# Latent attention with the keys on the partitions: scores made twice, sums taken by ones beside the values

## The chip, the cores and the metric

The kernel runs on one core of a Trainium2 chip. The metric is the device time of one execution in microseconds (us); the time of a kernel is the median of its runs. Engines are called PE (TensorE), PEld (its weight loads), DVE (VectorE), ACT (ScalarE), POOL (GpSimd) and SP (SyncE, which issues DMAs).

## The reference, cut to what matters

Two layers of a hybrid block run over 512 latent tokens and 256 context tokens of width 1024. In each layer an input projection is split into four head groups, each mixed in its own way; the four results are concatenated, projected out, normed and added, and a gated MLP follows. The change is in the fourth group, multi-head latent attention with 4 heads, 64 + 32 score features and 64 value features a head:

```python
def attend(q, k, v):
    ...
    def block(qblk):
        s = jnp.einsum('bqhd,bkhd->bhqk', qblk, k).astype(F32) * scale
        p = jax.nn.softmax(s, axis=-1).astype(v.dtype)
        return jnp.einsum('bhqk,bkhd->bqhd', p, v)
...
ox = attend(queries(cq_x, True), jnp.concatenate([kc, kx], axis=1), jnp.concatenate([vc, vx], axis=1))
if ctx_out:
    oc = attend(queries(cq_c, False), kc, vc).reshape(...)
```

The latent queries see all 768 keys, the context queries only the 256 context keys. Context outputs are made in the first layer (layer 0) and not in the second (layer 1).

## The kernel before, in words

Activations lie with features on the partitions and tokens in the free dimension. Tokens 0 to 511 are the latent stream (groups 0 and 1 of 256), tokens 512 to 767 the context (group 2). Large products are made of three float32r matmuls (`mm3`, L199 to L201): each operand is split into a high part and the rest, and high x high, low x high and high x low are summed in PSUM. Plain float32 matmuls are used elsewhere; the trace records each of them as two instructions with a weight load each, and a transpose through PE as one.

`mixer_d` is a generator called by `mixers`. Its first part makes the rotated shared keys, the values `V` (tile `dv`, tokens on the partitions, 256 columns for 4 heads) and, with `project(h)`, the split queries (`qh2`, `ql2`: slots of tile `hhx` for heads 0 and 1, tiles `pq` and `pl` for heads 2 and 3) and keys (`kh2`, `kl2` in tiles `hh` and `hl`, two slots, used again by heads 2 and 3). After the `yield` follow the four heads, with `project(2)` after head 0 and `project(3)` after head 1.

`attend(h, qt)` does one block of 128 queries: scores with the queries on the partitions (nine matmuls of 256 columns for a latent block, three for a context block), the maximum along the free dimension on DVE (L1136), the exponential on ACT with the maximum as bias and the sum accumulated (L1138), a reciprocal of 128x1 (L1140), transposes of the probabilities by PE (L1144), their copies out of PSUM by ACT (L1148) and DVE (L1146), the product with the values (L1151, 64 columns) and the scaling by the reciprocal (L1153). `finish(hp)` transposes the outputs of two heads back (L1163), splits them into `hhx` and `hlx` for the output projection (`parts`, L1192 and L1193) and stores the context part. `turn(w)` hands out PSUM tiles by turns: two of two banks (`pe2`, `pd2`) and four of one bank (`pe1` and `pd1`, two buffers each), the whole PSUM.

After the generator, `mixers` loads the results of the other three groups back from DRAM in three pieces through one buffer (`mix`, L1643) and splits them by the same `parts`. They may be split as soon as the last read of the queries of heads 0 and 1 has released `hhx` (`new_hx`, called after head 1). The output projection, with `pf` in PSUM, follows.

The order of instructions on each engine is set by the framework's scheduler: instructions whose inputs are ready in its own timeline are issued by priority, which follows program order, so that work of the next block fills gaps of the one before. Each engine then runs its list in that order and waits at the head of it.

## Time and profile before

| | us |
|---|---|
| median of 3 runs | 1920.27 |
| lowest, highest | 1911.92, 1923.88 |
| the profiled execution, device time | 1919.09 |
| its span in the profile | 1917.0 |
| PE busy (share) | 1777.0 (93%) |
| DVE busy (share) | 1197.3 (62%) |
| ACT busy (share) | 777.2 (41%) |
| mean granted clock of PE | 0.942 |

The profile is of one execution. A busy PE is not a PE at its peak: a row's duration holds the passage through the array, so the pace of a run of matmuls is read from the distance between their starts. The granted clock is a share of 2.4 GHz; 0.50 is the lower level, 1.2 GHz.

### The profile page before, as it was taken

The page shows a single profiled execution, that of the slowest core. Times are in us where ns is not written, and L with a number is a line of the kernel's source. Part 1 is how long each engine was busy: PE and PEld are TensorE (multiplying, and loading weights), DVE is VectorE, ACT ScalarE, POOL GpSimd, SP SyncE. Part 2 cuts the span into 40 slices and gives each one's busy share as a digit, 9 for nine tenths or more (in the row PEclk, how much of TensorE's full clock was granted, in tenths as well). Part 3 has the DMA queues.
Part 4 walks back from the last instruction along what each step waited for, and adds up shares of the span by engine and source line. Part 5 has one row for each costly group of instructions (what it writes and reads, how often), then busy time and mean ns, then how long its engine had stood idle before and what let it go on. Part 6 is the DMA issues. An engine that isn't in the chain of part 4 may idle for free.

```text
span 1917.0 us, 28265 instructions
## 1 busy us (share of the span) xinstructions
PE 1777.0 (93%) x11256; PEld 1523.2 (79%) x11256; DVE 1197.3 (62%) x2200; ACT 777.2 (41%) x1241; POOL 123.5 (6%) x142
## 2 busy tenths in 40 slices
PE   5899999889988999999999988988879999999996
PEld 2785777689977788888888887877669988888886
DVE  8866734655899744774683674792554665454545
ACT  3433454445653332322232354364434653333332
POOL 0000000001420000000000042000000320000002
PEclk9999998889999999999999978998788899999998
DMA  9457630006624332453442323322002622323241
GB/s 351 148 171 248 192 95 23 28 26 214 185 74 131 114 117 95 124 162 94 130 145 89 138 78 114 111 78 88 23 24 81 195 87 81 110 84 110 82 150 44
DMA packets 94387, 222.16 MB, mean 116 GB/s; under 512 B 10928, under 2 KB 41008, under 8 KB 93232
## 3 DMA queue, kind: packets, MB, share of 16 engines
q1 hardware_dynamic: 94256, 220.36, 36.7%
q8 instruction: 89, 1.46, 0.3%
q14 instruction: 42, 0.34, 0.1%
HBM read 193.35 MB, written 24.08 MB: 113 GB/s over the span
## 4 chain that ended last, share of the span: by engine, by line
PE 71%; DVE 12%; issue 10%; ACT 4%; DMA 2%; POOL 1%; SPq 0%; POOLq 0%; DVEq 0%; ACTq 0%
PE pf L199 16%; PE pf L200 16%; PE pf L201 16%; PE pg L199 3%; PE pg L201 3%; PE pg L200 3%; PE pb L243 1%; DVE wlo L192 1%; DVE z L1205 1%; PE pd L1151 1%; PE pn L322 1%; PE pc L704 1%; DVE nu L389 1%; DVE junk L236 1%; DMA bk<-bk 1%
## 5 line engine op out<-in xcount | busy, mean ns | idle before, releaser
L192 DVE TENSOR_TENSOR wlo<-raw,whi 128x1024 fp32r<-128x1024 f32 (+1 forms) x215 | 252.2, 1174 | 299.5 <-ACT whi L191 294.4
L191 ACT ACTIVATE whi<-raw 128x1024 fp32r<-128x1024 f32 (+1 forms) x215 | 217.2, 1011 | 399.4 <-PE pf L200 340.6
L199 PE MATMUL pf<-hhx,whi 128*128 128x512 f32 (+1 forms) x1032 | 363.5, 359 | 11.3 <-DVE z L1205 5.1
L200 PE MATMUL pf<-hlx,whi 128*128 128x512 f32 (+1 forms) x1032 | 368.1, 358 | 5.3 <-DVE hlx L391 5.0
L201 PE MATMUL pf<-hhx,wlo 128*128 128x512 f32 (+1 forms) x1032 | 365.3, 355 | 0.3 <-DVE wlo L192 0.3
L199 PEld LDWEIGHTS pf<-hhx,whi 128*128 128x128 f32 x1032 | 198.2, 195 | 39.3 <-ACT hhx L390 5.7
L200 PEld LDWEIGHTS pf<-hlx,whi 128*128 128x128 f32 x1032 | 200.6, 194 | 33.0 <-DVE hlx L391 8.4
L201 PEld LDWEIGHTS pf<-hhx,wlo 128*128 128x128 f32 x1032 | 200.6, 194 | 26.5 <-DVE wlo L192 0.5
L199 PE MATMUL pf<-g,whi 128*128 128x512 f32 (+1 forms) x552 | 185.4, 342 | 6.0 <-DVE z L1205 3.4
L201 PE MATMUL pf<-g,wlo 128*128 128x512 f32 (+1 forms) x552 | 187.3, 341 | 0.8 <-DVE wlo L192 0.8
L200 PE MATMUL pf<-g,whi 128*128 128x512 f32 (+1 forms) x552 | 187.6, 341 | 0.0
L1205 DVE SCALAR_TENSOR_TENSOR z<-pf,cols,z 128x511 f32<-128x511 f32 (+1 forms) x264 | 167.9, 656 | 24.3 <-ACT z L1203 21.7
L200 PE MATMUL pf<-hl,whi 128*128 128x256 f32 x432 | 123.5, 287 | 1.5 <-DVE hl L391 1.4
L199 PE MATMUL pf<-hh,whi 128*128 128x256 f32 x432 | 121.6, 286 | 1.7 <-ACT hh L390 1.7
L201 PE MATMUL pf<-hh,wlo 128*128 128x256 f32 x432 | 122.6, 285 | 0.0
L199 PEld LDWEIGHTS pf<-g,whi 128*128 128x128 f32 x552 | 104.7, 192 | 19.6 <-issue 4.3
L201 PEld LDWEIGHTS pf<-g,wlo 128*128 128x128 f32 x552 | 105.8, 192 | 12.2 <-DVE wlo L192 1.0
L200 PEld LDWEIGHTS pf<-g,whi 128*128 128x128 f32 x552 | 105.9, 192 | 11.3
L1203 ACT ACTIVATE z<-pf,cols 128x512 f32<-128x512 f32 (+1 forms) x132 | 89.8, 694 | 34.3 <-PE pf L201 29.3
L1284 DVE TENSOR_TENSOR y<-y,pf 128x512 f32<-128x512 f32 (+1 forms) x88 | 44.6, 515 | 73.8 <-PE pf L201 73.6
L125 POOL TENSOR_TENSOR nroy<-nroy,mhalf 128x2 f32<-128x2 f32 x10 | 9.9, 994 | 1211.4 <-DVE nroy L124 896.3
L200 PEld LDWEIGHTS pf<-hl,whi 128*128 128x128 f32 x432 | 83.4, 193 | 3.8 <-DVE hl L391 2.3
(457 smaller groups left out, 3434.1 us busy)
## 6 DMA issues: line engine op xcount, KB each, us to landing
raw<-in_w SPq DMA_DIRECT2D x170, 512.0 KB, 3.6
rawm<-in_wmod SPq DMA_DIRECT2D x64, 512.0 KB, 4.2
raw<-in_w SPq DMA_DIRECT2D x48, 384.0 KB, 3.1
wm<-in_wmod SPq DMA_DIRECT2D x8, 1024.0 KB, 10.1
silu<-in_wmod SPq DMA_DIRECT2D x16, 512.0 KB, 5.8
dx<-g SPq DMA_DIRECT2D x32, 256.0 KB, 2.2
dG<-gt SPq DMA_DIRECT2D x16, 256.0 KB, 2.3
dE<-es SPq DMA_DIRECT2D x16, 256.0 KB, 2.7
```

The source lines that it names most:

```text
L191: nc.scalar.activation(hv, src, AF.Copy)
L192: nc.vector.tensor_tensor(lv, src, hv.bitcast(F32), op=ALU.subtract)
L199: self.nc.tensor.matmul(out, lh, rh, start=i == 0, stop=False)
L200: self.nc.tensor.matmul(out, lh, rl, start=False, stop=False)
L201: self.nc.tensor.matmul(out, ll, rh, start=False, stop=i == n - 1)
L236: self.nc.vector.scalar_tensor_tensor(junk[:], wt, 1.0, self.silu[w][:], op0=ALU.mult, op1=ALU.mult, accum_out=self.modacc[l][:, w, m:m + 1])
L243: self.nc.tensor.matmul(acc[32 * q:32 * q + 2, :], self.ct[:, k, :], halves[q // 2][:, q % 2 * 512:q % 2 * 512 + 512], start=k == 0, stop= ...
L322: self.nc.tensor.matmul(ps[:, j:j + 1], acc[:, k, j * 128:(j + 1) * 128], self.ones[:, 0:1], start=k == 0, stop=k == 1)
L389: nc.vector.scalar_tensor_tensor(u[:], xk, sc, pb, op0=ALU.mult, op1=ALU.mult)
L1203: nc.scalar.activation(z[:, o:o + m], p[:, :m], AF.Identity, bias=b, scale=w1)
L1205: self.last = nc.vector.scalar_tensor_tensor(z[:, o + d:o + d + m - 1], p[:, s:s + m - 1], w, z[:, o + d:o + d + m - 1], op0=ALU.mult, op1 ...
L1284: nc.vector.tensor_tensor(y[:, m, t0:t0 + tw], y[:, m, t0:t0 + tw], ps[:, :tw], op=ALU.add)
```

## The change: what it does

- `attend` is replaced by `maxima(h)` and `values(h)`. `maxima` makes the scores as before, in pieces of 512 and 256 columns, and keeps only the negated maxima (DVE). It turns the six (or four) columns of maxima into one row by PE transposes of a column read 128 times, and writes that row, split into a high and a low part, into partition 96 of the queries. Partition 96 of the keys holds ones in the high part and zeros in the low.
- `values` makes the scores again with the keys on the partitions, 97 rows instead of 96, so that the maximum is subtracted by the matmul itself: per 128 keys three float32r matmuls of 512 queries (256 for context queries), one exponential on ACT, and one float32 matmul with `V` as weights. `V` has 192 columns for a pair of heads, 64 of one head, 64 ones, 64 of the other, so that 128 columns of it give the values in one half of the partitions and the sums of the probabilities in the other.
- After the last keys, DVE takes the reciprocal of the sums (64 partitions x 512) and multiplies. The result has features on the partitions, so the transposes of `finish` go away.
- The sums live in one PSUM bank `po` with one buffer; the one-bank tiles that are handed out by turns are three now instead of four (`pe1` has one buffer).
- New in the first part: a POOL memset for the ones in `V`, two copies instead of one for each piece of `V`, and two DVE copies that write ones and zeros into partition 96 of the keys.
- Order: `maxima` of heads 0 and 1, `values(0)`, `project(2)`, `maxima(2)`, `values(1)`, `project(3)`, `maxima(3)`, `finish(0)`, `values(2)`, `values(3)`, `finish(1)`.

```diff
--- before.py
+++ after.py
@@ -28,7 +28,7 @@
 CHUNKS = [6, 6, 6, 4]
 NCH = T // 8
 KDVE = 5
-PB = 3
+PB = 4
 XK, RK, KS = 4, 7, KT
 AHD = 0
 AHO = 0
@@ -85,7 +85,7 @@
 
 
 WU, NW = w_units()
-TAG_BUFS = {"pg": 2, "pb2": 1, "pb1": 2, "px2": 1, "pc1": 2, "pd2": 1, "pe2": 1, "pe1": 2, "pd1": 2, "pf": 6, "pn": 2, "pn4": 1, "pm": 3}
+TAG_BUFS = {"pg": 2, "pb2": 1, "pb1": 2, "px2": 1, "pc1": 2, "pd2": 1, "pe2": 1, "pe1": 1, "po": 1, "pd1": 2, "pf": 6, "pn": 2, "pn4": 1, "pm": 3}
 
 
 class Net:
@@ -1079,17 +1079,25 @@
         rotate(kr, ps)
         nc.scalar.copy(kr[r0, NX:], ps[r0, NX:T])
 
-        V = self.t(p, [128, 6, 256], "dv")
+
+        V = self.t(p, [128, 6, 2, 192], "dv")
+        nc.gpsimd.memset(V[:, :, :, 64:128], 1.0)
         for i in range(0, 6, 4):
             n = min(4, 6 - i)
             ps = self.turn(2)
             for j in range(n):
                 nc.tensor.matmul(ps[:, j * 256:(j + 1) * 256], ck[:96, (i + j) * 128:(i + j + 1) * 128],
                                  wk[:96, 256:512], start=True, stop=True)
-            nc.scalar.copy(V[:, i:i + n].rearrange("p i c -> p (i c)"), ps[:, :n * 256])
+            pv = ps[:, :n * 256].rearrange("p (i a r c) -> p i a r c", i=n, a=2, r=2)
+            for r in range(2):
+                nc.scalar.copy(V[:, i:i + n, :, r * 128:r * 128 + 64], pv[:, :, :, r, :])
         scale = float(96 ** -0.5)
         qs2 = [self.h_slots("hhx", F32R)[0]] * 2
         kh2, kl2 = (self.h2_slot(x) for x in ("hh2", "hl2"))
+
+        mrow = slice(96, 97)
+        for v, x in ((kh2, self.ones), (kl2, self.zeros)):
+            nc.vector.tensor_copy(v[mrow], x[mrow, 0:1].unsqueeze(2).to_broadcast([1, 2, T]))
 
         def project(h):
             hr = h % 2
@@ -1119,72 +1127,75 @@
 
         ot = {}
 
-        def attend(h, qt):
+        def maxima(h):
 
             hp, hr = h // 2, h % 2
-            qs = slice(qt * 128, (qt + 1) * 128)
-            kg = (0, 1, 2) if qt < 4 else (2,)
-            k0 = kg[0] * 256
-            nk = len(kg) * 256
-            ps = self.turn(2)
             qh2, ql2 = qs2[hp]
-            for g in kg:
-                gs = slice(g * 256, (g + 1) * 256)
-                self.mm3(ps[:, g * 256 - k0:g * 256 - k0 + 256],
-                         [((qh2[:96, hr, qs], ql2[:96, hr, qs]), (kh2[:96, hr, gs], kl2[:96, hr, gs]))])
-            mx = self.t(p, [128, 3], "dmx", bufs=4)
-            nc.vector.tensor_reduce(mx[:, 0:1], ps[:, :nk], axis=AX.X, op=ALU.max, negate=True)
-            pr, pp = (self.t(self.pe, [128, T], x, bufs=PB)[:] for x in ("pr", "pt"))
-            nc.scalar.activation(pr[:, :nk], ps[:, :nk], AF.Exp, bias=mx[:, 0:1],
-                                 accum_out=mx[:, 1:2])
-            nc.vector.reciprocal(mx[:, 2:3], mx[:, 1:2])
-            for a, b in ((0, 384), (384, 768)) if nk == 768 else ((0, 256),):
-                pt = self.turn(1)
-                for j in range(a, b, 128):
-                    nc.tensor.transpose(pt[:, j - a:j - a + 128], pr[:, j:j + 128], self.ident)
-                if a:
-                    nc.vector.tensor_copy(pp[:, a:b], pt[:, :b - a])
-                else:
-                    nc.scalar.copy(pp[:, a:b], pt[:, :b - a])
-            po = pt[:, 384:448]
-            for j in range(nk // 128):
-                nc.tensor.matmul(po, pp[:, j * 128:(j + 1) * 128], V[:, k0 // 128 + j, h * 64:h * 64 + 64],
-                                 start=j == 0, stop=j == nk // 128 - 1)
-            return ts(ot[hp][:, qt, hr * 64:hr * 64 + 64], po, mx[:, 2:3], None, op0=ALU.mult)
-
-        def heads(h):
+            mx = self.t(p, [128, 6], "dmx", bufs=2)
             for qt in range(nq):
-                attend(h, qt)
-
-        def finish(hp):
-
+                qs = slice(qt * 128, (qt + 1) * 128)
+                k0 = 0 if qt < 4 else 512
+                nk = T - k0
+                ps = self.turn(2)
+                for k1, w in ((0, 512), (512, 256))[qt // 4:]:
+                    gs = slice(k1, k1 + w)
+                    self.mm3(ps[:, k1 - k0:k1 - k0 + w],
+                             [((qh2[:96, hr, qs], ql2[:96, hr, qs]), (kh2[:96, hr, gs], kl2[:96, hr, gs]))])
+                nc.vector.tensor_reduce(mx[:, qt:qt + 1], ps[:, :nk], axis=AX.X, op=ALU.max, negate=True)
             ps = self.turn(2)
             for qt in range(nq):
-                nc.tensor.transpose(ps[:, qt * 128:(qt + 1) * 128], ot[hp][:, qt], self.ident)
+                nc.tensor.transpose(ps[:, qt * 128:(qt + 1) * 128], mx[:, qt:qt + 1].to_broadcast([128, 128]), self.ident)
+            nc.scalar.activation(qh2[mrow, hr, :tn], ps[mrow, :tn], AF.Copy)
+            tt(ql2[mrow, hr, :tn], ps[mrow, :tn], qh2[mrow, hr, :tn].bitcast(F32), op=ALU.subtract)
+
+        def values(h):
+
+            hp, hr = h // 2, h % 2
+            qh2, ql2 = qs2[hp]
+            rows, other = slice(hr * 64, hr * 64 + 64), slice(64 - hr * 64, 128 - hr * 64)
+            for q0, nqs, kts in ((0, 512, range(6)), (512, 256, (4, 5)))[:2 if ctx_out else 1]:
+                qs = slice(q0, q0 + nqs)
+                po = self.t(self.pso, [128, 512], "po")
+                for j in kts:
+                    ks = slice(j * 128, (j + 1) * 128)
+                    ps = self.turn(1)
+                    self.mm3(ps[:, :nqs], [((kh2[:97, hr, ks], kl2[:97, hr, ks]), (qh2[:97, hr, qs], ql2[:97, hr, qs]))])
+                    pt = self.t(self.pe, [128, 512], "pt", bufs=PB)
+                    nc.scalar.activation(pt[:, :nqs], ps[:, :nqs], AF.Exp)
+                    nc.tensor.matmul(po[:, :nqs], V[:, j, hp, hr * 64:hr * 64 + 128], pt[:, :nqs],
+                                     start=j == kts[0], stop=j == 5)
+                rec = self.t(self.pe, [128, 512], "rec", bufs=2)
+                nc.vector.reciprocal(rec[rows, :nqs], po[other, :nqs])
+                tt(ot[hp][rows, qs], po[rows, :nqs], rec[rows, :nqs], op=ALU.mult)
+
+        def finish(hp):
+
             for g in range(2):
                 gs = slice(g * 256, g * 256 + 256)
-                self.parts(g, slice(6 + hp, 7 + hp), ps[:, gs].unsqueeze(1))
+                self.parts(g, slice(6 + hp, 7 + hp), ot[hp][:, gs].unsqueeze(1))
             if ctx_out:
-                mix = self.t(p, [128, T], "df")
-                nc.scalar.copy(mix[:, NX:], ps[:, NX:T])
-                store(hp, mix, NX)
+                store(hp, ot[hp], NX)
 
         for h in range(2):
             project(h)
         yield
-        ot[0] = self.t(p, [128, 6, 128], "dot")
-        heads(0)
+        ot[0] = self.t(self.pe, [128, T], "dot", bufs=2)
+        for h in range(2):
+            maxima(h)
+        values(0)
         qs2[1] = [self.t(self.pe, [128, 2, T], x, F32R) for x in ("pq", "pl")]
         project(2)
-        heads(1)
+        maxima(2)
+        values(1)
         self.new_hx()
         for g in range(2):
             self.new_h(g)
         project(3)
+        maxima(3)
         finish(0)
-        ot[1] = self.t(self.pe, [128, 6, 128], "dot")
+        ot[1] = self.t(self.pe, [128, T], "dot", bufs=2)
         for h in (2, 3):
-            heads(h)
+            values(h)
         finish(1)
 
     def parts(self, g, ks, src):
@@ -1635,7 +1646,8 @@
         mxs.__exit__(None, None, None)
         psls.__exit__(None, None, None)
         with self.pool("pse", space=PSUM) as pse, self.pool("me") as self.pe:
-            self.psd = {2: [(pse, "pe2"), (psd, "pd2")], 1: [(pse, "pe1"), (psd, "pd1")]}
+            self.psd = {2: [(pse, "pe2"), (psd, "pd2")], 1: [(pse, "pe1"), (psd, "pd1"), (psd, "pd1")]}
+            self.pso = pse
             next(d, None)
             self.pre = [self.load_w(l, ("out", j), i) for j in range(2) for i in range(2)]
             for k in range(0, 6, 2):
```

## Rows read from the trace of the kernel before

**Rows 1.** The page: busy time of an engine, and the chain by engine.
```profile
PE 1777.0 (93%) x11256; PEld 1523.2 (79%) x11256; DVE 1197.3 (62%) x2200; ACT 777.2 (41%) x1241; POOL 123.5 (6%) x142
...
PE 71%; DVE 12%; issue 10%; ACT 4%; DMA 2%; POOL 1%; SPq 0%; POOLq 0%; DVEq 0%; ACTq 0%
```

**Rows 2.** Stretches: length; PE, PEld, DVE, ACT, POOL busy (instructions); clock; DMA share, GB/s.
```profile
308.00:354.90 46.90, 40.05 (x378) 27.62 (x377) 28.54 (x51) 19.15 (x36) 0.00 (x0) 0.67 0.09 30
...
354.90:440.10 85.20, 76.40 (x543) 70.26 (x541) 50.03 (x110) 41.50 (x92) 0.00 (x0) 0.90 0.07 21
1345.00:1396.50 51.50, 41.77 (x437) 29.46 (x435) 31.52 (x60) 18.72 (x35) 0.61 (x2) 0.73 0.05 17
...
1396.50:1471.40 74.90, 65.08 (x447) 59.34 (x448) 41.24 (x82) 30.48 (x62) 0.00 (x0) 0.85 0.08 25
...
415.00:420.00 5.00, 5.00 (x25) 5.00 (x25) 0.64 (x3) 0.43 (x3) 0.00 (x0) 0.50 0.00 0
```

**Rows 3.** Waits, 355 to 440 then 1395 to 1475: total, times, longest.
```profile
PE pe L1144 <- ACT pr L1138: 6.3, 4, 2.8
...
ACT hhx L1192 <- DMA mix<-dmixr: 2.4, 2, 1.6
...
PE pe L1144 <- ACT pr L1138: 8.9, 4, 2.8
...
ACT hhx L1192 <- DMA mix<-dmixr: 5.3, 2, 4.3
```

**Rows 4.** Timeline of PE in the MLP, first and last of two runs of 18.
```profile
701.84 0.40 PE L199 MATMUL pf<-g,whi 128*128 128x512 f32 x1
...
705.72 0.39 PE L201 MATMUL pf<-g,wlo 128*128 128x512 f32 x1
705.94 0.28 PE L199 MATMUL pf<-g,whi 128*128 128x256 f32 x1
...
707.98 0.28 PE L201 MATMUL pf<-g,wlo 128*128 128x256 f32 x1
```

**Rows 5.** Chain of waits in order of time, layer 0's attention: start, us, what.
```profile
383.52 0.33 PE pe L1144 x3
...
386.27 2.63 PE pd L1151 x24
...
389.81 1.43 PE pe L1099 x4
...
392.34 2.60 PE pd L1111 x8
```

**Rows 6.** DVE by line and shape: busy us, mean ns, idle before.
```profile
L1146 DVE COPY pt<-pd 128x384 f32<-128x384 f32 x32 | 17.7, 552 | 13.4 <-PE pd L1144 13.3
L1136 DVE TENSOR_REDUCE dmx<-pe 128x1 f32<-128x768 f32 x16 | 15.3, 954 | 8.7 <-PE pe L201 8.6
...
L1072 DVE TENSOR_TENSOR hlx<-pd,dcst 32x512 f32<-32x512 f32 x10 | 7.0, 696 | 0.1
L1140 DVE RECIPROCAL dmx<-dmx 128x1 f32<-128x1 f32 x40 | 6.4, 159 | 6.8 <-ACT pr L1138 6.7
L764 DVE COPY s5a<-s5v 64x512 f32<-64x512 f32 x8 | 4.7, 593 | 0.0
...
L947 DVE TENSOR_TENSOR bon<-bon,bry 128x1536 f32<-128x1536 f32 x1 | 1.8, 1757 | 0.0
...
L528 DVE RECIPROCAL eq<-eq 128x32 f32<-128x32 f32 x2 | 0.7, 344 | 0.0
...
L527 DVE TENSOR_TENSOR eq<-eq,ks 128x32 f32<-128x32 f32 x2 | 0.4, 192 | 0.0
```

**Rows 7.** ACT by line and shape, the same columns.
```profile
L1148 ACT COPY pt<-pe 128x384 f32<-128x384 f32 x32 | 15.2, 476 | 27.2 <-PE pe L1144 26.8
L1138 ACT ACTIVATE pr<-pe,dmx 128x768 f32<-128x768 f32 x16 | 14.4, 900 | 18.4 <-DVE dmx L1136 18.1
...
L806 ACT ACTIVATE s5a<-pc,s5hb 128x512 f32<-128x512 f32 x4 | 2.7, 687 | 7.7 <-PE pc L804 7.7
```

## The prediction

> **What bounds the kernel now.** I read the page first: PE is busy 93% of the span and holds 71% of the chain that ended last, DVE 12% [rows 1]. So a change counts by what it does to PE's time, as work or as waiting. Next come the stretches that attention covers [rows 2]: 85.2 us in layer 0 (354.9 to 440.1, first scores to the first output projection) and 74.9 us in layer 1 (1396.5 to 1471.4). The two are 160 us, 8.3% of the time. PE is idle in them for 85.20 - 76.40 = 8.8 and 74.90 - 65.08 = 9.8 us. The mean granted clock is 0.90 and 0.85, that is 17 and 22 us at the lower level (1.2 GHz), and half of that is lost: 8.5 and 11.2 us. Losses in all: 17.3 + 21.0 us. The waits say where the idle time arises [rows 3]: PE waits at the transposes for exponentials, four times a layer, up to 2.8 us. ACT in turn stands at the head of its list waiting for the DMA of `mix`, 2.4 us in layer 0 and 5.3 us in layer 1. After such gaps PE stays at 0.50 for long: from 415 to 420 it was busy all the time and was still granted the lower level [rows 2].
>
> **PE's work, warm.** The paces: a float32r matmul of 512 columns takes (705.72 - 701.84)/17 = 0.228 us, one of 256 (707.98 - 705.94)/17 = 0.120 us [rows 4]. Transposes go at 0.33/3 = 0.11 us, the product with the values at 2.63/24 = 0.110 us an instruction (its 64 columns take as long as a transpose's 128, so the weight load sets that pace). `project`'s eight query instructions, four of 512 and four of 256, take 2.60 us: 0.433 and 0.217 us each [rows 5]. These last are the price of the new float32 product, which streams 512 columns in two instructions.
>
> Per head in layer 0, before: 42 score matmuls 5.04, 28 transposes 3.08, 56 product instructions 6.14, 3 transposes of `finish` 0.33; sum 14.6 us. After: `maxima` 4 x 3 x (0.228 + 0.120) + 2 x 3 x 0.120 = 4.90, six transposes 0.66, second scores 18 x 0.228 + 6 x 0.120 = 4.82, product 12 x 0.433 + 4 x 0.217 = 6.06; sum 16.4. That is +1.8 a head, +7.3 for the layer. In layer 1, without context queries: 12.4 before (4.32 + 2.64 + 5.26 + 0.22), 13.9 after (4.18 + 0.44 + 4.10 + 5.20), +5.9 for the layer. **PE gains 13.2 us of work.** As a check on the paces: layer 0's four heads and the two projections inside (each 1.3 for keys, from the 1.43 of the row, and 2.6) come to 66.2 us warm; 85.2 less this is 19.0 us lost, near the 17.3 above.
>
> **The other engines.** Removed on DVE: 40 small reciprocals, 32 copies of 0.55, 40 scalings. On ACT, 40 sums and 40 copies of up to 0.48 go away, and the exponential of 0.90 per 128 latent queries [rows 6, 7]. Added on ACT: 48 exponentials of 128x512 at 0.69, 8 of half that width, and a row copy a head; ACT gets lighter. Its 0.69 per 128 keys lies beside 3 x 0.228 + 2 x 0.433 = 1.55 us of PE, so with three score tiles by turns it is hidden; without this cover it would add about 0.7 us 24 times a layer. DVE keeps the maxima, 0.95 per block [rows 6], against 1.04 us of PE: balanced, two tiles by turns.
>
> **The reciprocal of 64x512** is the operation that no row shows. Lower bound: a pass over 512 elements from PSUM, 0.70 us. The rows that are the same operation: 128x1 takes 159 ns, 128x32 344 ns, while a tensor_tensor of 128x32 takes 192 [rows 6]. So the reciprocal costs (344 - 159)/31 = 6.0 ns an element and 512 of them 0.159 + 511 x 0.006 = 3.2 us; 256 take 1.7. I take 3.2, since it is the same operation in the same kernel. By the Trainium skill ("VectorE: DVE Perf Modes", First, the fixed hardware budget) the reciprocal is an iterative divide with a repeat count of 8; read as eight cycles an element at the 0.96 GHz that the skill states, 512 would take an estimated 4.3 us, and the sum below would rise by about 5 us. Row 128x32 would then be over 0.4 us; it is 0.344, and the measurement stands.
>
> What waits: `po` has one buffer, so the next product into it waits for reciprocal, product and semaphores: 3.2 + 0.7 + 0.2 = 4.1 us after a latent part, 2.3 after a context part. Behind the waiting matmul all of PE is queued; on DVE, the next maxima and the splits of `project` stand behind the reciprocal. What covers it: three score tiles ahead (2.05 us), the second projections (3.9 us) and later `maxima`. Of eight hand-overs in layer 0 and four in layer 1 about half are covered; I count 5 us for each layer, between 0 and 11.
>
> **The stretches after.** Layer 0: work 73.5 (65.7 + 7.8). Start: 5 us (as now, the idle time until the second projection is evacuated and some clock, with 1.5 more because the first maxima are bound by DVE). Waits behind `mix`, which are still at the same place in ACT's list: 4 (now about 5, with more work ready on PE), 2.5 for the clock after them, since runs of 512 columns follow instead of 64-column products. Hand-overs 5. Sum 90.0, +4.8. Layer 1: work 60.6 (55.6 + 6.1, less 1.1 of scores that run before), start 3, `mix` 4, clock 2.5, hand-overs 5: 75.1, +0.2. The tail costs nothing extra in this, as the output projection has seven of eight input tiles ready; if the scheduler puts the eighth early in PE's list it costs up to 2.4 us in each layer.
>
> **Before the stretches.** Writing ones and zeros into partition 96 takes two DVE copies of 1536 elements: 64x512 takes 0.59 and a 1536-wide pass 1.76 [rows 6], so 1.5 to 1.8 each, two a layer. DVE is busy 28.5 of 46.9 and 31.5 of 51.5 us there [rows 2], in a chain that alternates between PE and DVE, so I count half of the 6.4 us, 3 (0 to 6.4). The POOL memset is covered by an idle POOL, the extra copies of `V` by ACT (19 of 47 us busy); uncovered they are about 1 us each.
>
> Sum: 4.8 + 0.2 + 3 = +8.0 us against the profiled execution's 1919.09, 1927.1. The median of the runs lies 1.2 above that execution, so **1928 us**.
>
> **Rivals.**
> *The hand-over of `po` decides (slower).* If the scheduler's timeline takes the reciprocal for an ordinary pass, it puts the next product 2.5 us too early in PE's list and nothing fills the gap. Layer 0: four latent hand-overs of 4.1 less 0.7 of context scores, 13.6; layer 1: three of 4.1 - 2.05 and a tail of 4.9 - 2.5, 8.6. That is 12 above the 10 counted; each gap of over 2.5 us also drops the clock, an estimated 2 us each (after the 5 us at 0.50 of [rows 2]), six times: 8 + 12 + 12 = +32, 1952. It decides from 3 us of reciprocal on. For it: the rows of the reciprocal. Against it: under the same scheduler PE is busy 76.4 of 85.2 us [rows 2].
> *The stalls go (no change, or a little faster).* ACT has half the work here and `maxima` needs nothing of it; if the waits behind `mix` are covered and the clock holds, 13 us of the forecast's losses and 6 us of hand-overs vanish: 8 - 19 = -11, 1909. Over 1% faster would need nearly all of the 38 us of losses to go while 13 us of work are added. For it: PE's waits of [rows 3] are all on exponentials. Against it: the DMA wait itself stays.
> *The reciprocal at 512 wide costs an ordinary pass.* 3.2 becomes 0.7, hand-overs are covered: 8 - 10 = -2, 1918. Against it: the two rows of different width.
>
> **How the numbers follow.** About 1% (19 us) is what a measurement here can tell from no change. Forecast 0.50, with its own range 1917 to 1939; hand-over 0.22; stalls gone 0.20; cheap reciprocal 0.08. Faster by over 1% comes from a quarter of the stalls case: 0.05. Slower by over 1% from most of the hand-over case and a tenth of the forecast: 0.20. The rest, 0.75, is the same. The range reaches from the stalls case to most of the hand-over case: 1908 to 1948.
>
> **What would show it.** The reciprocal's row at 64x512: near 3.2 us. The second scores at 0.228 and the product at 0.433 us an instruction. PE busy in the stretches up by some 13 us at a better clock, its idle time moved from the transposes (waiting for ACT) to the product into `po` (waiting for DVE). Stretches of 90 and 75 us. Wrong would make me: a reciprocal of under 1 us, an exponential that PE waits for at every 128 keys, or a start of the stretches that comes over 6 us later because of DVE.

## The result and the profile after

The changed kernel takes 1964.53 us (median of 4 runs, 1959.53 to 1968.68) beside 1920.12 for the kernel before (4 runs on the same chip): ratio 1.0225, 95% interval 1.02 to 1.0249, slower by 44 us where 8 were forecast. The profiled execution took 1965.26 us, its span is 1963.4.

The page of the changed kernel, the two lines that answer to [rows 1]:

```profile
PE 1804.6 (92%) x10836; PEld 1506.5 (77%) x10836; DVE 1217.5 (62%) x2124; ACT 758.3 (39%) x1187; POOL 125.2 (6%) x144
...
PE 67%; DVE 14%; issue 10%; ACT 4%; DMA 3%; POOL 1%; SPq 1%; POOLq 0%; DVEq 0%; ACTq 0%
```

PE lost four points of the chain and DVE gained two. To see where the time lies, the span is cut at marks that both kernels have: the first rotated key of a layer (tile `brs`) and the first matmul of the output projection (`pf`). First the kernel before, then the changed one (columns as in [rows 2]):

```profile
311.69:440.09 128.40, 112.75 (x876) 95.20 (x876) 76.27 (x157) 58.45 (x123) 0.00 (x0) 0.81 0.08 25
1352.75:1471.44 118.69, 99.14 (x764) 82.60 (x765) 69.19 (x137) 46.70 (x93) 0.00 (x0) 0.78 0.06 19
```

```profile
315.71:464.89 149.18, 125.62 (x664) 86.35 (x665) 86.66 (x114) 48.73 (x90) 0.00 (x0) 0.80 0.07 21
1387.54:1515.50 127.96, 109.77 (x557) 71.16 (x557) 69.49 (x99) 39.95 (x75) 0.00 (x0) 0.79 0.06 17
```

Of the 46.4 us that the span grew, 20.8 lie in the stretch of layer 0 and 9.3 in that of layer 1: 30.1 in latent attention. The stretch from the projection to layer 1 grew by 7.3, the ones ahead of the two marks by 5.9 and 2.7, the end by 2.3; the beginning lost 1.8. Those other parts are taken up at the end of the experiments.

What the operations cost, DVE then ACT, columns as in [rows 6]:

```profile
L1168 DVE RECIPROCAL rec<-po 64x512 f32<-64x512 f32 x8 | 26.8, 3355 | 25.3 <-PE po L1165 25.2
L1168 DVE RECIPROCAL rec<-po 64x256 f32<-64x256 f32 x4 | 7.0, 1754 | 3.4 <-PE po L1165 3.3
L1169 DVE TENSOR_TENSOR dot<-po,rec 64x512 f32<-64x512 f32 x8 | 5.5, 686 | 0.2
L1144 DVE TENSOR_REDUCE dmx<-pe 128x1 f32<-128x768 f32 x16 | 15.3, 955 | 24.8 <-PE pe L201 24.7
L1100 DVE CAST hl<-zeros 1x1536 fp32r<-1x1536 f32 x2 | 1.9, 956 | 0.3 <-PE pg L200 0.2
...
L1164 ACT ACTIVATE pt<-pd 128x512 f32<-128x512 f32 x32 | 18.3, 595 | 11.0 <-PE pd L201 10.5 <-PE po L1165 0.3
```

The reciprocal is what it was priced at, 3.36 and 1.75 us. The largest waits of PE in layer 0's attention (350.6 to 464.9), in place of those for exponentials in [rows 3]:

```profile
PE pd L199 <- DVE dmx L1144: 5.7, 4, 2.9
PE po L1165 <- DVE dot L1169: 5.4, 4, 4.3
PE pe L199 <- DVE dmx L1144: 3.7, 3, 2.2
PE pd L199 <- ACT df L1124: 2.7, 1, 2.7
PE pd L1119 <- DVE hhx L1149: 2.0, 1, 2.0
```

All of these but one are for DVE, 16.8 us; the one for ACT is the first row of the window, ahead of the first scores, and is as long without a division (2.72 us in `e1_copy` below). Of the 16.8, some 3.6 (2.16, 1.05 and 0.41 us) come before the first reciprocal. The timeline of DVE in the same stretch shows what stood ahead of those maxima and splits (start, us, engine, line, operation; in brackets the engine's idle time before it and who ended it):

```profile
389.56 3.36 DVE L1168 RECIPROCAL rec<-po 64x512 f32<-64x512 f32 x1 [3.09 <-PE po L1165]
392.95 0.96 DVE L1149 TENSOR_TENSOR hhx<-pd,hhx 1x768 fp32r<-1x768 f32 x1
...
409.96 3.35 DVE L1168 RECIPROCAL rec<-po 64x512 f32<-64x512 f32 x1 [0.73 <-PE po L1165]
413.35 0.96 DVE L1144 TENSOR_REDUCE dmx<-pe 128x1 f32<-128x768 f32 x1
...
436.93 3.36 DVE L1168 RECIPROCAL rec<-po 64x512 f32<-64x512 f32 x1
440.32 0.96 DVE L1144 TENSOR_REDUCE dmx<-pd 128x1 f32<-128x768 f32 x1
...
459.18 3.35 DVE L1168 RECIPROCAL rec<-po 64x512 f32<-64x512 f32 x1 [9.81 <-PE po L1165]
```

And PE in the same stretch:

```profile
393.97 2.85 PE L1119 MATMUL pd<-cq,dwq 128*128 128x512 f32 x8 [2.00 <-DVE hhx L1149]
...
414.36 0.39 PE L199 MATMUL pe<-hh,pq 96*128 96x256 f32 x1 [2.21 <-DVE dmx L1144]
...
441.34 0.58 PE L199 MATMUL pd<-hh,pq 96*128 96x256 f32 x1 [2.89 <-DVE dmx L1144]
...
463.41 2.04 PE L1165 MATMUL po<-pt,dv 128*128 128x256 f32 x4 [4.26 <-DVE dot L1169]
```

Each of the four 512-wide reciprocals of layer 0 has its gap on PE. Three times it is not the next product into `po` that waits, but a score tile or a row split whose small operation stood behind the reciprocal in DVE's list. Only the last, at 463.41, is a long wait for the hand-over of `po` itself (the other three for `po` are 1.2 us together): the context product of head 3 stands ahead of the output projection in PE's list and waits for the one buffer.

### The profile page after: what moved, and what is told of

Read it like the earlier page. It is cut to its first block, busy times and chain, and to the rows that moved or that the text cites. A ratio compares the mean times of both kernels' runs of the same rounds, so it can differ in the third digit from the quotient of the medians.

```text
span 1963.4 us, 27222 instructions
## 1 busy us (share of the span) xinstructions
PE 1804.6 (92%) x10836; PEld 1506.5 (77%) x10836; DVE 1217.5 (62%) x2124; ACT 758.3 (39%) x1187; POOL 125.2 (6%) x144
## 4 chain that ended last, share of the span: by engine, by line
PE 67%; DVE 14%; issue 10%; ACT 4%; DMA 3%; POOL 1%; SPq 1%; POOLq 0%; DVEq 0%; ACTq 0%
PE pf L199 16%; PE pf L200 16%; PE pf L201 15%; PE pg L199 3%; PE pg L201 3%; PE pg L200 3%; DVE wlo L192 1%; PE pb L243 1%; PE po L1165 1%; DMA raw<-in_w 1%; DVE rec L1168 1%; DVE z L1216 1%; PE pn L322 1%; DMA bk<-bk 1%; ACT whi L191 1%
## 5 line engine op out<-in xcount | busy, mean ns | idle before, releaser
L1216 DVE SCALAR_TENSOR_TENSOR z<-pf,cols,z 128x511 f32<-128x511 f32 (+1 forms) x264 | 168.0, 656 | 24.2 <-ACT z L1214 21.7
L201 PE MATMUL pf<-hh,wlo 128*128 128x256 f32 x432 | 123.0, 286 | 0.0
```

Of the source, the lines that this page charges most:

```text
L201: self.nc.tensor.matmul(out, ll, rh, start=False, stop=i == n - 1)
L1216: self.last = nc.vector.scalar_tensor_tensor(z[:, o + d:o + d + m - 1], p[:, s:s + m - 1], w, z[:, o + d:o + d + m - 1], op0=ALU.mult, op1 ...
```

## The experiments

The main theory, A: the length of the reciprocal on DVE holds PE back, by the one buffer of `po` (A1) or by what stands behind it in DVE's list (A2). A3 says that DVE's time counts wherever it stands. Rivals: B, the doubled scores, that is PE's own work; C, waits for the DMA of `mix`; D, the maxima, which DVE makes slower than PE makes the scores. Each time below is a median; "layer 0" and "layer 1" are the stretches cut as above, of one profiled execution. Such a stretch holds whatever clock was granted in that execution: c2's layer 1 is 13 us shorter than those of c4 and c7, while the three medians lie within 3 us (see there).

| kernel | us | ratio to before, 95% interval | layer 0 | layer 1 |
|---|---|---|---|---|
| before | 1920.1 | | 128.4 | 118.7 |
| changed | 1964.5 | 1.0225 (1.02 to 1.0249) | 149.2 | 128.0 |
| e1_copy: no division | 1928.4 | 1.0048 (1.0023 to 1.0073) | 128.7 | 120.2 |
| e3_evac: `po` copied out at once | 1961.1 | 1.0215 (1.0178 to 1.0253) | 147.0 | 129.5 |
| e2_two_po: two buffers of `po` | 1949.8 | 1.0155 (1.0121 to 1.0189) | 142.5 | 124.6 |
| e5_blocks: shorter division | 1942.5 | 1.0113 (1.0075 to 1.015) | 132.0 | 121.3 |
| e8_behind: e3, reciprocals behind the maxima | 1927.4 | 1.0048 (1.0018 to 1.0078) | 130.6 | 121.4 |
| e7_pin: order on DVE alone | 1948.2 | 1.0154 (1.011 to 1.0199) | 142.3 | 126.6 |
| e9_pin_two: e7 with two buffers | 1941.3 | 1.0123 (1.0069 to 1.0178) | 140.6 | 123.9 |
| c1_one: e5, maxima from one matmul | 1914.8 | 0.9963 (0.9937 to 0.9988) | 126.4 | 110.8 |
| c2_two: c1, high row only, two buffers | 1907.3 | 0.993 (0.9905 to 0.9955) | 123.0 | 99.7 |
| c3_evac: c1, high row only, `po` copied | 1925.3 | 1.0034 (1.001 to 1.0059) | 124.1 | 115.2 |
| c4_order: c2, maxima of head 1 later | 1910.1 | 0.994 (0.9918 to 0.9962) | 123.4 | 113.3 |
| c7_pin: c2, pinned | 1906.9 | 0.9938 (0.9918 to 0.9958) | 122.7 | 112.6 |
| c5_behind: e8, one matmul, high row | 1922.9 | 1.001 (0.9991 to 1.0029) | 124.4 | 110.9 |
| c6_behind_blocks: c5, shorter division | 1915.5 | 0.9977 (0.9953 to 1.0001) | 120.9 | 107.9 |

**e1_copy, the length of the reciprocal.** A plain copy stands in its place, so the division is left out.

```diff
-                nc.vector.reciprocal(rec[rows, :nqs], po[other, :nqs])
+                nc.vector.tensor_copy(rec[rows, :nqs], po[other, :nqs])
```

> The reciprocal of the 64x512 (and 64x256) sums becomes a plain DVE copy of the same tile, so the division is left out; nothing else is edited. Theory A (the length of the reciprocal on DVE, 3.36 and 1.75 us by the trace of the changed kernel, holds back PE: directly where the next product waits for `po`, and through the maxima, row splits and query splits that stand behind it in DVE's list): each of the 8 + 4 operations falls to about 0.65 and 0.4 us, 27 us less on DVE; the 15.8 us of them on layer 0's chain of waits and about as much in layer 1 mostly go, some clock with them: 20 to 30 us off 1964.5, 1935 to 1945. The waits of PE for `dot` and for maxima of over 2 us vanish. Theory B (the doubled scores, that is PE's own work, and the start of attention at half clock with two score tiles): these stay, so no more than 5 us off, 1960 or over. Theory C (waits for the DMA of `mix` and the clock after them): 0 to 5 us off.

36 us less, more than A said, 28.2 of it in the two stretches (20.5 and 7.8), and B and C fall as causes of it: doubled scores, three score tiles, `mix` and the start are all still there, and the stretches are back at the lengths of the kernel before (+0.3 and +1.5 us). The stretches of this run:

```profile
317.88:446.61 128.73, 115.13 (x664) 77.78 (x665) 71.90 (x114) 48.51 (x90) 0.00 (x0) 0.89 0.08 24
1362.75:1482.94 120.19, 107.03 (x556) 69.91 (x557) 61.21 (x99) 40.08 (x75) 0.00 (x0) 0.80 0.06 18
```

Beside the changed kernel layer 0 is 20.5 us shorter: PE is idle for 13.6 us instead of 23.6, and its same 664 instructions are busy for 115.1 us instead of 125.6, at a granted clock of 0.89 instead of 0.80. So in layer 0 half of what the reciprocals cost is idle time and half is a lower clock. In layer 1 it is 5.0 us of idle time and 2.7 of busy time. That the gaps lowered the clock is likely, but not shown: with other lists idle time and clock did not move together (`e7_pin` and `e9_pin_two` below).

**e3_evac and e2_two_po, the buffer of `po` alone.**

```diff
-                nc.vector.reciprocal(rec[rows, :nqs], po[other, :nqs])
-                tt(ot[hp][rows, qs], po[rows, :nqs], rec[rows, :nqs], op=ALU.mult)
+                ev = self.t(self.pe, [128, 512], "ev", bufs=2); nc.scalar.copy(ev[:, :nqs], po[:, :nqs]); nc.vector.reciprocal(rec[rows, :nqs], ev[other, :nqs])
+                tt(ot[hp][rows, qs], ev[rows, :nqs], rec[rows, :nqs], op=ALU.mult)
```

> As soon as the product is complete ACT copies `po` (128x512) into SBUF, about 0.6 us; reciprocal and multiplication read that copy. So `po` comes free after about 0.8 us in place of 4.1, while DVE's list keeps the whole reciprocal. Theory A1 (PE loses the time at the one buffer of `po`): the direct waits of PE for `dot` (4.26 us at the tail, 4.7 + 0.7 in all) and the order that the scheduler arranged around the late buffer go, 10 us or more off 1964.5: under 1955. Theory A2 (the time is lost in DVE's list, where maxima and splits stand behind the reciprocal): the maxima still wait 2.2 to 2.9 us each; less than 6 us off: 1958 to 1965. Theory B (PE's work): no change, 1962 to 1967.

3 us less, 0.7 of it in the two stretches: A1 alone falls. The first line is this run's stretch of layer 0. In PE's timeline below it the tail's wait shrank from 4.26 to 0.68, and the waits behind DVE's list stayed or grew:

```profile
310.47:457.48 147.01, 125.52 (x665) 84.76 (x665) 82.62 (x111) 51.38 (x95) 0.00 (x0) 0.80 0.07 21
...
407.84 0.58 PE L199 MATMUL pd<-hh,pq 96*128 96x256 f32 x1 [3.15 <-DVE dmx L1144]
411.12 0.47 PE L1147 MATMUL pe<-cst,dmx 128*128 128x128 f32 x1 [1.21 <-DVE dmx L1144]
...
441.16 1.54 PE L1147 MATMUL pd<-cst,dmx 128*128 128x128 f32 x6 [2.60 <-DVE dmx L1144]
...
456.70 1.13 PE L1165 MATMUL po<-pt,dv 128*128 128x256 f32 x4 [0.68 <-ACT ev L1168]
```

```diff
-TAG_BUFS = {..., "pe1": 1, "po": 1, ...}
+TAG_BUFS = {..., "po": 2, ...}
-            self.psd = {..., 1: [(pse, "pe1"), (psd, "pd1"), (psd, "pd1")]}
+            self.psd = {..., 1: [(psd, "pd1")]}
```

> `po` gets two buffers; the bank comes from `pe1`, so two one-bank score tiles go by turns instead of three. The reciprocal is as it was. Theory A1 (one buffer of `po`): 8 to 15 us off 1964.5, less what the third score tile was worth; the tail's wait of 4.26 us for `dot` goes. Theory A2 (DVE's list): within 5 us of 1964.5, and if the third score tile covered the exponential (0.6 us beside 1.55 us of PE for 128 keys) up to 5 us slower. Theory B: 1962 to 1970.

15 us less, 10.1 of it in the two stretches, with two score tiles in place of three. That isn't the buffer alone: the scheduler's list came out otherwise, with the row split of head 1 ahead of the first reciprocal, and the wait of 2.00 us for it is gone along with the tail's. So these two runs leave open how buffer and order share the loss.

**e8_behind, the order of DVE's list.** `e3_evac` with the reciprocals and multiplications of heads 0 and 1 written after `maxima(2)` and `maxima(3)`:

```diff
...
+                ev = self.t(self.pe, [128, 512], "ev", bufs=4); nc.scalar.copy(ev[:, :nqs], po[:, :nqs]); later.append((ev, rows, other, qs, nqs, ot[hp]))
+        def norm():
+            while later:
+                ev, rows, other, qs, nqs, o = later.pop(0)
+                rec = self.t(self.pe, [128, 512], "rec", bufs=2)
+                self.tc.keep_in_program_order(nc.vector.reciprocal(rec[rows, :nqs], ev[other, :nqs]))
+                tt(o[rows, qs], ev[rows, :nqs], rec[rows, :nqs], op=ALU.mult)
...
         maxima(2)
+        norm()
...
         maxima(3)
+        norm()
...
             values(h)
+            norm()
```

> As the run in which ACT copies `po` (1961.1 us), with one edit more: the reciprocals and their multiplications are written after the maxima of the next head (heads 0 and 1) and pinned on DVE behind all that was written before them. DVE does the same operations of the same length (3.35 us), but no maxima stand behind a reciprocal any more. Theory A2 (PE loses its time at maxima and row splits that stand behind the reciprocal in DVE's list: 3.15, 1.21, 1.83, 0.97, 2.60 and 1.81 us in layer 0 of that run, 11.6 in all, and about 6 in layer 1, and some clock with them): 10 to 18 us off 1961, 1943 to 1951, less what the splits of `project(3)` and `finish(0)` lose by standing behind two reciprocals now. Theory A3 (it is the sum of DVE's time, wherever it stands): no change, 1957 to 1964.

The same operations of the same length as in `e3_evac`, and 34 us less: as fast as with no division at all (1927.4 and 1928.4). In the two stretches it is 16.4 + 8.1 = 24.5 us, and PE's list hardly differs there in layer 0 (251 of the 260 rows of its timeline from the first scores on stand in the same order). That is A2. The rest of the 34 lies outside, above all between layer 0's projection and layer 1, where DVE's list came out otherwise (see the end of the experiments). DVE's timeline now has all maxima and the row split ahead of the reciprocal:

```profile
408.88 0.42 DVE L1144 TENSOR_REDUCE dmx<-pd 128x1 f32<-128x256 f32 x1
410.65 0.96 DVE L1149 TENSOR_TENSOR pl<-pe,pq 1x768 fp32r<-1x768 f32 x1 [1.35 <-ACT pq L1148]
411.64 3.35 DVE L1174 RECIPROCAL rec<-ev 64x512 f32<-64x512 f32 x1
```

The stretches show the same two halves as above: in layer 0 PE is idle for 13.9 us instead of 21.5 and busy for 116.7 instead of 125.5, at a clock of 0.87 instead of 0.80; over both layers the gaps give 12.2 us, less than the 17.6 that A2 counted, and the busy time 12.2 more.

```profile
319.45:450.03 130.58, 116.72 (x665) 79.83 (x665) 82.34 (x111) 51.38 (x95) 0.00 (x0) 0.87 0.08 24
1360.21:1481.64 121.43, 107.66 (x556) 71.22 (x557) 69.57 (x99) 42.08 (x78) 0.00 (x0) 0.79 0.06 18
```

**e7_pin and e9_pin_two, order without the copy.** In the changed kernel only the reciprocal is pinned behind what was written before it; then the same with the two buffers of `e2_two_po`.

```diff
-                nc.vector.reciprocal(rec[rows, :nqs], po[other, :nqs])
+                self.tc.keep_in_program_order(nc.vector.reciprocal(rec[rows, :nqs], po[other, :nqs]))
```

> The changed kernel with one edit: each reciprocal is pinned on DVE behind all that was written before it. The operations, their lengths and the one buffer of `po` are as they were (1964.5 us); what changes is the order of DVE's list (the row split of head 1 and four of the six maxima of head 2 stand ahead of the reciprocals now, two of the six of head 3 still stand behind one), and with it the scheduler's places of a few products on PE. Theory A2 alone (the order of DVE's list is the cause, whatever `po` does): the waits of 2.00, 2.21 and part of 2.89 us in layer 0 and 2.73, 2.88 in layer 1 go, 10 to 20 us off: 1944 to 1954. Theory A1+A2 (a reciprocal of 3.36 us must stand somewhere: with one buffer it holds either the maxima or the next product): the waits move to the products into `po`, under 6 us off or slower: 1958 to 1970.

> The same pin and two buffers of `po` (two score tiles): 1949.8 us without the pin. Theory A1+A2: the reciprocal then holds neither, and the time comes down to that of the runs without a division and with the reciprocals behind (1927 to 1930), or within 6 us of it: 1925 to 1936. Theory A2 alone: as with the pin alone, less the tail's 4.26 us. Theory that only the length counts: no change from 1949.8.

Order alone gives 16 us in the median, within A2's bounds, but only 8.3 of it lie in the two stretches. Two of the six maxima of head 3 and the row behind them still follow a reciprocal here, and the tail is as it was:

```profile
429.87 0.58 PE L199 MATMUL pd<-hh,pq 96*128 96x256 f32 x1 [3.29 <-DVE dmx L1144]
434.58 1.54 PE L1147 MATMUL pd<-cst,dmx 128*128 128x128 f32 x6 [2.84 <-DVE dmx L1144]
...
453.21 1.66 PE L1165 MATMUL po<-pt,dv 128*128 128x256 f32 x4 [4.26 <-DVE dot L1169]
```

With two buffers it is 23 us, less than the 28 or more that A1+A2 said (its four runs spread from 1934 to 1952, and the stretches in the table are of the slowest one). Their stretches of layer 0, `e7_pin` first:

```profile
312.06:454.31 142.25, 119.61 (x665) 81.80 (x665) 86.78 (x114) 48.26 (x90) 0.00 (x0) 0.85 0.07 22
316.97:457.54 140.57, 125.24 (x665) 85.87 (x665) 82.81 (x111) 48.30 (x88) 0.00 (x0) 0.79 0.07 22
```

The pin alone leaves 22.6 us of idle time and a better clock (0.85); pin and buffers leave 15.3, near `e8_behind`, at 0.79. So what sets the clock is not the idle time of the stretch alone, and stays open. Put together, medians first, then the two stretches: the place in `po` alone 3 and 0.7 us, the order alone 16 and 8.3, both 23 and 12.7 (`e9_pin_two`) to 37 and 25.1 (`e8_behind`), the last where no maxima stand behind a reciprocal. Either one alone leaves most of the loss.

**e5_blocks, a shorter division.** The sums are the same in 64 partitions, so after a transposition of blocks of 32x32 one column of each block holds 32 different sums:

```diff
-                nc.vector.reciprocal(rec[rows, :nqs], po[other, :nqs])
...
+                nc.vector.transpose(sm[rows, :nqs], po[other, :nqs])
+                nc.vector.reciprocal(rc[rows, :nqs // 32], sm[rows, :nqs:32])
+                nc.vector.transpose(rec[rows, :nqs].rearrange("p (b c) -> p b c", c=32), rc[rows, :nqs // 32].unsqueeze(2).to_broadcast([64, nqs // 32, 32]))
```

> The division stays, over fewer elements: DVE transposes the sums in blocks of 32x32 (each block row is a repeated value, so that after it a column of each block holds 32 different sums), takes the reciprocal of 64x16, and transposes it back, read 32 times, to 64x512. I expect about 0.7 + 0.25 + 0.65 = 1.6 us on DVE in place of 3.36 (1.0 for 1.75); no row so far shows the block transposes. Theory A (reciprocal's length): a bit over half of what leaving the division out gives, 12 to 18 us off 1964.5: 1947 to 1953. Theory B or C: 0 to 4 us off.

22 us less, 23.9 in the two stretches, a little more than A said. Its DVE rows give 0.714 + 0.245 + 0.704 = 1.66 us in place of 3.36:

```profile
L1168 DVE STREAM_TRANSPOSE sm<-po 64x512 f32<-64x512 f32 x8 | 5.7, 714 | 24.2 <-PE po L1165 21.0 <-PE pd L1147 3.2
L1168 DVE STREAM_TRANSPOSE rec<-rc 64x512 f32<-64x512 f32 x8 | 5.6, 704 | 0.2
...
L1168 DVE RECIPROCAL rc<-sm 64x16 f32<-64x16 f32 x8 | 2.0, 245 | 0.2
```

**c1_one and c2_two, the price of the doubled scores, and a faster kernel.** Both with the block transposes; `c2_two` has c1's edit, the second one here (without the zeros in the keys, too), and e2's two buffers:

```diff
-                    self.mm3(ps[:, k1 - k0:k1 - k0 + w],
-                             [((qh2[:96, hr, qs], ql2[:96, hr, qs]), (kh2[:96, hr, gs], kl2[:96, hr, gs]))])
+                    nc.tensor.matmul(ps[:, k1 - k0:k1 - k0 + w],
+                                     qh2[:96, hr, qs], kh2[:96, hr, gs], start=True, stop=True)
```

```diff
...
-            tt(ql2[mrow, hr, :tn], ps[mrow, :tn], qh2[mrow, hr, :tn].bitcast(F32), op=ALU.subtract)
...
-                    self.mm3(ps[:, :nqs], [((kh2[:97, hr, ks], kl2[:97, hr, ks]), (qh2[:97, hr, qs], ql2[:97, hr, qs]))])
+                    for i, (x, y, r) in enumerate(((kh2, qh2, 97), (kh2, ql2, 96), (kl2, qh2, 96))):
+                        nc.tensor.matmul(ps[:, :nqs], x[:r, hr, ks], y[:r, hr, qs], start=i == 0, stop=i == 2)
```

> The block transposes of the earlier run (1942.5 us), and `maxima` makes its scores of the high parts alone, one matmul in place of three; the maximum is only a shift and cancels between values and sums, so nothing is left out of the result. This takes 24.2 us of warm PE work away (layer 0: 4 heads x (8 x 0.348 + 4 x 0.120) = 13.1; layer 1: 4 x 8 x 0.348 = 11.1). Theory B (the doubled scores, as PE work, set the time once the reciprocal is short): 20 us off or more, 1915 to 1923. Theory D (DVE's maxima, 0.95 us a block beside 0.35 us of PE, bound that part, above all at the start where nothing else is there for PE, and the new gaps cost clock): 5 to 14 us off, 1928 to 1938.

> As the run before, and the row of maxima is used in its high part alone (no split on DVE, 0.96 or 0.70 us eight times; no zeros in the keys, 0.95 us twice), the second scores' two small products over 96 rows; and `po` has two buffers, with two score tiles. Theory A1 (what is left of the hand-over, 2.65 us at the tail with the block transposes): 4 to 8 us under the run before: 1922 to 1932. If the third score tile covers the exponential: no better than the run before.

The single matmul gives 28 us in the median, as B said and beyond D. But in the two stretches it is 5.7 + 10.5 = 16 us of the 24.2 of warm work, between D and B; 9 more lie between layer 0's projection and layer 1 (845.6 and 836.5 us), where the code of the two is the same and DVE's list is not. So once the reciprocal is short, PE's work counts at about two thirds of its length in the stretches that hold it. `c2_two` is faster than both kernels, 0.7% under the kernel before:

```profile
315.32:438.35 123.03, 108.72 (x584) 70.38 (x583) 70.84 (x120) 49.01 (x88) 0.00 (x0) 0.79 0.08 25
1354.40:1454.08 99.68, 82.62 (x493) 50.55 (x493) 60.95 (x101) 40.38 (x75) 0.00 (x0) 0.90 0.07 22
```

**c3_evac, c4_order, c7_pin, variants of it.** c3 is c2 with `po` copied out by ACT as in e3, one buffer, three score tiles; c4 is c2 with `maxima(1)` written after `values(0)`; c7 is c2 with the first block transpose pinned.

> As the run before, but three score tiles and one `po`, which ACT copies out at once (0.59 us), so that the block transposes and the multiplication read SBUF. Theory A1: within 3 us of the run with two buffers, since the wait for `po` at the tail falls from 2.65 to 0.7 us. ACT's eight copies a layer cost nothing as long as PE doesn't wait for exponentials.

> As the run with two buffers of `po` (1907.3 us), but the maxima of head 1 are written after the second scores of head 0, so that they can fill in beside them. Theory D (DVE's maxima bound the start, where PE has no other work): the second scores of head 0 start up to 4 us earlier and the maxima of head 1 lie beside them: 2 to 5 us off, 1902 to 1905. If the scheduler's list is nearly the same as before: 1905 to 1910.

> The fastest kernel so far (block transposes, maxima from the high parts alone, two buffers of `po`, 1907.3 us) with the first block transpose pinned in the same way. With 1.7 us in place of 3.36 there is little to win by order: PE waited for maxima behind such work no longer than 1.2 us there. 1903 to 1909.

The medians of c4 and c7 can't be told from c2's, as was expected of c7 and half expected of c4: with DVE's work short, these two changes of order decide nothing. c3 missed: 18 us over c2, and no cause is shown. Its layer 1 is 15.5 us longer than c2's, with a lower clock ahead of the maxima there (the first 30 us or so of the stretch, c2, c3, c4, c7):

```profile
1354.00:1385.00 31.00, 22.98 (x305) 15.86 (x304) 23.99 (x43) 16.35 (x33) 0.00 (x0) 0.96 0.01 2
1363.00:1395.00 32.00, 29.05 (x302) 20.05 (x300) 18.89 (x34) 14.56 (x30) 0.00 (x0) 0.73 0.01 2
1357.00:1388.00 31.00, 29.95 (x247) 20.41 (x246) 16.86 (x31) 12.82 (x27) 0.00 (x0) 0.56 0.01 2
1352.70:1383.00 30.30, 29.25 (x234) 19.88 (x236) 16.86 (x31) 12.80 (x27) 0.00 (x0) 0.55 0.01 1
```

But c4 and c7, as fast as c2 in the median, have a lower clock still and a layer 1 of 113.3 and 112.6 us, within 3 us of c3's. So it is c2's layer 1 that stands out, in its profiled and fastest execution (1901.6 us), and the difference in layer 1 is no account of c3's median. 6 us of the 18 lie between layer 0's projection and layer 1. Why the clock differs in instructions that these kernels share stays open.

**c5_behind and c6_behind_blocks, does a reciprocal cost nothing where nobody stands behind it?** `e8_behind` with c2's maxima and rows; then also with the block transposes.

> As the run with the long reciprocals pinned behind the next maxima (1927.4 us; ACT copies `po`), with maxima from the high parts alone and the row used in its high part alone. Theory A2 (a reciprocal of 3.35 us costs nothing where nobody stands behind it): the gain of the single matmul, 1942.5 - 1914.8 = 28 us, comes on top, 1895 to 1905, no slower than the kernels with block transposes. Theory A3 (DVE's time counts wherever it stands; DVE now has 20 us of reciprocals in layer 0 beside a PE with 13 us less to do): 1908 to 1920.

> As the run before, with block transposes and a reciprocal of 64x16 in place of the long one, in the same place of DVE's list. Theory A2: within 4 us of the run before. Theory A3: 6 to 12 us under it (12 operations shorter by 1.7 and 0.7 us: 16 us of DVE).

A2 in that strict form missed by 18 us: c5 took 1922.9, and shorter reciprocals in the same place took 7 us off it, so A3 holds for a part. In the stretches the single matmul gave 6.2 + 10.6 us, as in c1, and the shorter division 3.5 + 3.0. The rest of c5's miss is outside the stretches: 9.5 us of it between layer 0's projection and layer 1 (836.8 in `e8_behind`, 846.3 here), again where the code is the same and DVE's list is not.

**Outside the stretches.** From layer 0's projection to layer 1 (the last gate logarithm, L842) the kernels took between 836.5 and 848.7 us: before 837.8, changed 845.1, e1 837.1, e3 848.7, e8 836.8, c5 846.3. From the same instruction in layer 0 to its first rotated key it was 85.5 before, 85.6 to 86.2 in e2, e3, e7 and c7, and 89 to 92 in the changed kernel and the others. Neither goes with the edits; of the change, the POOL memset and the two casts (1.9 us a layer) lie ahead of the keys. The first goes in part with the order that the scheduler chose for instructions that no edit touches: from 20 to 260 us after the first `pf` matmul, DVE's list has another order in e3, e5, c3, c5 and c6 (at most 362 of some 415 instructions stand in the order of c2) than in the rest (391 or more), and these five take 845.6 to 848.7 us, the rest 836.5 to 842.2. The changed kernel does not fit: 845.1 with the order of the rest. So most of 16 us of the 46 of the span is not explained by a step of the change, and no run separates it. The times of two kernels can differ by 9 to 12 us through this alone (e5 and c1, e8 and c5, e3 and e8).

## Why the prediction was wrong, point by point

**The step that failed** is the price of the hand-overs: "about half are covered; I count 5 us for each layer, between 0 and 11". Against the run without a division they cost 20.5 us in layer 0 and 7.8 in layer 1, 28 where 10 were counted. The sentence ahead of it names what was behind the reciprocal ("on DVE, the next maxima and the splits of `project`"), but only the wait for `po` was priced. The runs show that this part can't be left out: freeing `po` alone gave 0.7 us of the 28, the order of DVE's list alone 8.3, both 25. And 13 of the 28 are longer busy time of the same instructions of PE, 10.5 of them in layer 0 at a clock of 0.80 for 0.89; the forecast had given the hand-overs no clock. The span grew by 46 us where 8 were forecast: 18 of these 38 are this term, 7 the other terms of the two layers, 13 lie outside the stretches and stay open.

**The rival that came nearest** said +32, 1952, for another reason: the next product too early in PE's list. The reciprocal did come out above its 3 us (no run tests that limit itself), and its 12 us of lost clock are near the 13 above, though no run shows that the gaps caused them; its place was wrong, since freeing `po` alone gave 3 us of the median. Nor does the scheduler take the reciprocal for an ordinary pass: with the copy in its place the context products of head 0 moved up in PE's list. The rival in which the stalls go is out: PE's idle time in the stretch of layer 0 rose from 15.7 to 23.6 us. The forecast's range ended 16 us below the result.

**Right:** the reciprocal at 3.2 and 1.7 us by the two rows of [rows 6] (3.36 and 1.75 measured; the third rival, a cheap one, is out). By the Trainium skill ("VectorE: DVE Perf Modes", First, the fixed hardware budget) the estimate was 4.3 us; the measurement decides. The exponential, priced at 0.69 and measured at 0.595, is hidden, and 128 keys take PE the 1.55 us that were worked out, as its timeline shows:

```profile
452.58 1.02 PE L1165 MATMUL po<-pt,dv 128*128 128x512 f32 x2
...
454.14 1.02 PE L1165 MATMUL po<-pt,dv 128*128 128x512 f32 x2
...
455.69 1.02 PE L1165 MATMUL po<-pt,dv 128*128 128x512 f32 x2
```

PE is busy in the two stretches of `e1_copy` for 10.3 us more than before (222.2 against 211.9), where 13.2 were worked out warm. A start that comes over 6 us later because of DVE, one of the signs of being wrong, did not show either: from the rotated key to the first scores of layer 0 it is 34.9 us in both the changed kernel and `e1_copy`, 43.2 before.

**Wrong in size:** without hand-overs the terms of the two layers came to 4.8 + 0.2 - 10 = -5, and `e1_copy` stands at +1.8, so they were together about 7 us too low. They are not told apart, and the cuts differ: the forecast's begin at the first scores, the measured ones at the rotated keys. In layer 0 of `e1_copy` PE has no wait of 0.4 us or more for an exponential, so the 4 us behind `mix` did not come as idle time; waits for maxima did, 5.3 us. The casts into partition 96 took 0.95 and 0.96 us each, not 1.5 to 1.8. **Wrong:** that the tail "costs nothing extra". Layer 0's tail has a gap of 4.26 us, since the context product stands ahead of the output projection and needs `po`.

## What to carry to other kernels

An operation on an engine that works its list in order is priced by what stands behind it in that list as well as by who waits for its result: the reciprocals, on an engine that was busy for 58% of the stretch, cost their own length in layer 0 (20.5 us for 20.4 us of reciprocals) and over half of it in layer 1 (7.8 for 13.4), in gaps and in a lower clock. Look in such a list for short operations on the critical path that stand behind a long one, and move the long one as well as freeing its buffer: either alone left most of the loss here. And a maximum that is only subtracted need not be exact: one matmul of three gave 16 us in the two stretches. Last, an edit can turn the scheduler's order of instructions far from it, so read an effect in the stretch that it touches and not from the whole time alone.

## What the runs showed of the hardware

- A DVE reciprocal costs (3355 - 1754)/256 = 6.25 ns for each further element from 256 to 512 a partition, and takes as long from PSUM as from SBUF (3347 ns in `e3_evac`).
- A DVE transposition of 32x32 blocks takes 0.714 us for 64x512 from PSUM and 0.448 for 64x256, within 6% of the multiplication of the same size (0.686 and 0.422), also where its input is a column read 32 times (0.704).
- A DVE cast of 1536 elements on one partition took 0.96 us. The 1536-wide pass by which it was priced, a tensor_tensor with two inputs over 128 partitions, takes 1.76 [rows 6].
- The granted clock can differ a lot between kernels in a stretch whose code is nearly the same: 0.96, 0.73, 0.56 and 0.55 over the first 30 us or so of layer 1's stretch in c2, c3, c4 and c7. No run shows what decides it.
